# A scan mixer's decay masks from one exponential instead of two, with its vector operands in PSUM

## Chip, cores, metric

One core of a Trainium2 chip runs the whole program. The metric is the device time of one execution in microseconds (us), the median of several runs. Engine names are those of the profile: PE multiplies matrices, PEld loads its weights, DVE is the vector engine, ACT the scalar engine, POOL the GpSimd engine, SP issues DMAs. SBUF is the on-chip memory, PSUM the eight banks of 128 x 512 float32 words that PE writes.

## What is computed

A four-layer trunk over 256 context tokens and 256 latent tokens, model width 1024. Each layer has a mixer and a gated feed-forward block (FFN); mixers are differential attention (layers 0 and 3), windowed attention (layer 1) and a bidirectional state-space scan (layer 2), which the change is about. Cut to that scan, for one direction:

```
xbc = silu(conv5(u @ w_xbc) + bias);  dt = softplus(u @ w_dt + dt_bias)
a_cs = cumsum(dt * A) over each chunk of 128 tokens
chunk_states = einsum(B, exp(a_cs[-1] - a_cs), x * dt)
state = state * exp(a_cs[-1]) + chunk_states
decay_in = exp(where(tril, a_t[..., :, None] - a_t[..., None, :], -inf))
y_diag = einsum(C @ B^T, decay_in, x * dt);  y_off = einsum(C, prev_state, exp(a_cs))
y = (y_forward + flip(y_backward) + x * d_skip) * silu(z)
out = rmsnorm_per_group(y) @ w_out
```

There are 32 heads of width 64 in 4 groups, state width 128, and four chunks (two per stream), forward and backward.

## The kernel before

Every large product is made to float32 accuracy from three matmuls (`lin`, L291 to L293): a weight tile is loaded by SP into `wr`, copied by ACT to `wh` (L264) and its rest is subtracted by POOL into `wl` (L266). A unit of the scan's projection is 24 matmuls of 512 columns into one PSUM bank (tag `mm`).

`ssd_mixer` (L1287) goes over four groups g. In each it makes ten units: two for B and C, four for x (all six go through `conv_silu`, L1076) and four gates z (`gate`, L1310). `conv_silu` copies the bank into the padded tile `xpad` (ACT, L1083), makes the first tap from it (ACT, L1089), adds four taps on DVE (L1097) in an SBUF tile `cw`, and ends with a tanh (ACT, L1100) and a product (DVE, L1102). The steps sizes dt are made once, in `ssd_dt` (L1126), which comes after the latent stream's gates and B, C units; its DVE chain (L1132 to L1146) ends in transposes on PE (L1152).

`ssd_core` (L1181) is called twice per group, for four heads each. It makes x by tokens (`xtok`, L1208); six weighted copies of it (DVE, L1222), from which PE makes the chunk states (L1227, recurrence on DVE, L1232 and L1236); a selector `sel` per direction (DVE, L1213). Then for each of two pairs of heads j, for each head and direction: PE spreads a row of cumulative sums over all partitions (`rb`, L1247), ACT subtracts the token's own sum and clips it by Relu (four instructions, L1256) and takes the exponential (L1259), DVE multiplies by `cd` (L1260), which POOL has made as score x dt (L1250). DVE adds the two directions (L1262), and PE makes the output from it (`yd`, L1266). The states' part is a product and an addition on DVE (L1284, L1285).

The order on each engine is set at build time by a scheduler from the program's order and its own costs, and each engine then runs its list in order. PSUM tags here: `mm` has two banks, to which `ar` is added while no FFN table is in it, and the bank `ad` goes to the tag named by `EXTRA`; `sc` has two, `sm` two. The four tiles `wa` are used by no one in this mixer; the next FFN block's first table rows are loaded into them ahead of it.

Of the kernel before, what the change touches and what calls it, by code (L numbers as in the profile page):

```python
# [180 lines left out]
class Trunk:  # L181
# [4 lines left out]
    DMB = 3  # L186
# [442 lines left out]
    def ffn(self, i, u, streams, pool, gate, after, nxt):  # L629
# [446 lines left out]
    def conv_silu(self, ps, ci, dst, s, pool):  # L1076
# [9 lines left out]
        acc = self.t([P, 2, HALF], "cw", self.CW, pool=pool)[:, :ns]  # L1086
# [5 lines left out]
        if self.ACTTAP:  # L1092
            tm = self.t([P, 2, HALF], "cw", self.CW, pool=pool)[:, :ns]
            nc.scalar.activation(tm, xp[:, s0:s1, 4 : 4 + HALF], AF.Copy, scale=tap(4))
            nc.gpsimd.tensor_tensor(out=acc, in0=acc, in1=tm, op=AL.add)
        for j in range(1, 5 - self.ACTTAP):
# [29 lines left out]
    def ssd_dt(self, ps, pool):  # L1126
# [4 lines left out]
        v, e, q, p = w(), w(), w(), w()  # L1131
# [49 lines left out]
    def ssd_core(self, g, hf, bc, xf, sc, pool):  # L1181
# [33 lines left out]

        prev = [{}, {}]
        for d, order in ((0, (0, 1, 2, 3)), (1, (1, 0, 3, 2))):
            hd = slice(32 * d + h0, 32 * d + h0 + 4)
            st = None
            for n, c in enumerate(order[:3]):  # L1220
                xw = self.t([P, HALF], "v", 4, pool=pool)
                tt(  # L1222
                    out=xw.rearrange("p (h x) -> p h x", h=4), in0=xtok[:, c].rearrange("p (h x) -> p h x", h=4),
                    in1=self.wst[:, c, hd].unsqueeze(2).to_broadcast([P, 4, 64]), op=AL.mult,
                )
# [14 lines left out]
        for j in range(2):  # L1240
            yd = self.psum("sc")
            for hh in (2 * j, 2 * j + 1):
                ms = []
                for d in range(2):
                    hd = 32 * d + h0 + hh
                    rb = self.psum("sc")
                    nc.tensor.matmul(rb, sel[d][:, hh, :], self.rows, start=True, stop=True)  # L1247
                    m = self.t([P, NT], "dm", self.DMB, pool=pool)
                    cd = self.t([P, NT], "cd", self.CDB, pool=pool)
                    getattr(nc, self.ENG_CD).tensor_tensor(  # L1250
                        out=cd.rearrange("p (c l) -> p c l", c=4), in0=cbm[d].rearrange("p (c l) -> p c l", c=4),
# [279 lines left out]
```

## Time and profile before

| what | us |
|---|---|
| median of 3 runs (2724.1 to 2736.1) | 2726.4 |
| the profiled execution: its own time | 2728.9 |
| its span in the profile | 2726.7 |
| PE busy | 2531.5 (93%) |
| DVE busy | 1648.1 (60%) |
| ACT busy | 1234.0 (45%) |
| POOL busy | 1089.7 (40%) |

The mixer of the change lies between about 1360 and 1870 us of the span. The shares above are averages over all layers; for this change the stretches of that mixer are read by themselves. A matmul's duration in the profile includes the time in which the next one already runs, so the pace of PE is read from the starts of successive matmuls.

### The profile page before, as it was taken

How to read it: one execution, taken by the hardware profiler on the slowest of the kernel's cores; microseconds unless marked ns; L12 is line 12 of the kernel's file. 1: busy time of each engine (PE TensorE's matmuls, PEld its weight loads, DVE VectorE, ACT ScalarE, POOL GpSimd, SP SyncE). 2: the span in 40 equal slices, each digit the busy share in tenths (PEclk: the TensorE clock that was granted, in tenths of full speed). 3: DMA queues.
4: the chain of work that ended last, by engine and by line, in shares of the span. 5: the costliest groups of instructions: out<-in, count | busy, mean ns of one | idle time of the engine just before them, and what ended most of it. 6: DMA issues, size and time to landing. Idle time of an engine off the chain costs nothing.

```text
span 2726.7 us, 37430 instructions
## 1 busy us (share of the span) xinstructions
PE 2531.5 (93%) x13570; PEld 2089.7 (77%) x13570; DVE 1648.1 (60%) x3844; ACT 1234.0 (45%) x2514; POOL 1089.7 (40%) x525
## 2 busy tenths in 40 slices
PE   7899999999999999999988888889999998997998
PEld 4777688888776798888876666667988887876997
DVE  3776649931567649921689898866485116667112
ACT  5454553222557653222545565554432225555543
POOL 3322044444321054444243445442544443433784
PEclk9999999999999999999989899999999999999999
DMA  8333437742231147732221111123486323323452
GB/s 319 116 102 122 149 99 260 255 151 93 94 101 47 46 140 263 265 113 94 99 86 39 56 53 60 65 77 108 142 299 239 99 94 104 105 88 130 147 185 78
DMA packets 108040, 353.29 MB, mean 130 GB/s; under 512 B 14032, under 2 KB 24656, under 8 KB 105808
## 3 DMA queue, kind: packets, MB, share of 16 engines
q1 hardware_dynamic: 107280, 349.57, 38.1%
q8 instruction: 107, 1.75, 0.3%
q10 hardware_dynamic: 576, 1.34, 0.1%
q14 instruction: 77, 0.63, 0.1%
HBM read 329.36 MB, written 11.53 MB: 125 GB/s over the span
## 4 chain that ended last, share of the span: by engine, by line
PE 67%; DVE 14%; ACT 5%; issue 3%; DMA 2%; POOL 2%; DVEq 0%; ACTq 0%; SPq 0%; POOLq 0%
PE mm L291 6%; PE mm L292 6%; PE mm L293 6%; PE sc L291 5%; PE sc L293 5%; PE sc L292 5%; PE mm L302 4%; PE mm L303 4%; PE mm L301 4%; DVE dm L1260 2%; DVE cw L1097 2%; PE sc L303 1%; PE sc L301 1%; PE sc L302 1%; POOL wl L266 1%
## 5 line engine op out<-in xcount | busy, mean ns | idle before, releaser
L266 POOL TENSOR_TENSOR wl<-wr,wh 128x1024 fp32r<-128x1024 f32 x356 | 856.1, 2411 | 1354.9 <-ACT wh L264 1216.2
L264 ACT ACTIVATE wh<-wr 128x1024 fp32r<-128x1024 f32 x356 | 377.0, 1061 | 756.8 <-issue 277.1
L291 PE MATMUL mm<-uh,wh 128*128 128x512 f32 (+1 forms) x1136 | 406.5, 358 | 9.0 <-ACT uh L560 8.4
L293 PE MATMUL mm<-uh,wl 128*128 128x512 f32 (+1 forms) x1136 | 406.0, 357 | 0.0
L292 PE MATMUL mm<-ul,wh 128*128 128x512 f32 (+1 forms) x1136 | 405.4, 357 | 0.5 <-DVE sublng L861 0.4
L644 DVE TENSOR_TENSOR sc<-sc,sg 128x512 f32<-128x512 f32 (+1 forms) x100 | 57.5, 575 | 430.0 <-PE sc L293 423.2
L291 PE MATMUL sc<-uh,wh 128*128 128x512 f32 (+1 forms) x800 | 273.0, 341 | 0.7 <-DVE hid L647 0.7
L293 PE MATMUL sc<-uh,wl 128*128 128x512 f32 (+1 forms) x800 | 272.4, 341 | 0.0
L292 PE MATMUL sc<-ul,wh 128*128 128x512 f32 (+1 forms) x800 | 272.4, 340 | 0.0
L291 PEld LDWEIGHTS mm<-uh,wh 128*128 128x128 f32 x1136 | 219.6, 193 | 41.3 <-ACT uh L560 9.0
L292 PEld LDWEIGHTS mm<-ul,wh 128*128 128x128 f32 x1136 | 219.2, 193 | 30.2 <-issue 2.5
L293 PEld LDWEIGHTS mm<-uh,wl 128*128 128x128 f32 x1136 | 219.2, 193 | 27.8 <-issue 1.8
L303 PE MATMUL mm<-wl,hid 128*128 128x512 f32 x444 | 176.1, 397 | 0.0
L301 PE MATMUL mm<-wh,hid 128*128 128x512 f32 x444 | 176.1, 397 | 0.0
L302 PE MATMUL mm<-wh,hid 128*128 128x512 f32 x444 | 175.8, 396 | 0.0
L291 PEld LDWEIGHTS sc<-uh,wh 128*128 128x128 f32 x800 | 152.2, 190 | 17.7 <-DVE hid L647 0.9
L292 PEld LDWEIGHTS sc<-ul,wh 128*128 128x128 f32 x800 | 151.9, 190 | 16.8
L293 PEld LDWEIGHTS sc<-uh,wl 128*128 128x128 f32 x800 | 151.9, 190 | 16.9
L390 DVE SCALAR_TENSOR_TENSOR sq<-wa,sm 128x512 f32<-128x512 f32 x224 | 145.1, 677 | 0.1
L266 POOL TENSOR_TENSOR wl<-wa,wh 128x1024 fp32r<-128x1024 f32 x49 | 117.9, 2406 | 56.4 <-ACT wh L264 56.0
L1250 POOL TENSOR_TENSOR cd<-h,dtt 128x512 f32<-128x512 f32 x64 | 78.6, 1233 | 123.7 <-DVE dm L1260 117.6
L291 PE MATMUL ar<-uh,wh 128*128 128x256 f32 (+1 forms) x352 | 120.6, 343 | 0.0
(415 smaller groups left out, 5735.0 us busy)
## 6 DMA issues: line engine op xcount, KB each, us to landing
wr<-in_fin SPq DMA_DIRECT2D x154, 512.0 KB, 3.5
wa<-in_adat SPq DMA_DIRECT2D x144, 512.0 KB, 4.8
wr<-in_fout SPq DMA_DIRECT2D x77, 512.0 KB, 3.5
wr<-in_ssi SPq DMA_DIRECT2D x40, 512.0 KB, 3.5
wa<-in_adaw SPq DMA_DIRECT2D x36, 512.0 KB, 5.3
wr<-in_daqk SPq DMA_DIRECT2D x24, 512.0 KB, 3.7
wa<-in_fin SPq DMA_DIRECT2D x22, 512.0 KB, 3.5
wr<-in_sso SPq DMA_DIRECT2D x16, 512.0 KB, 3.5
```

Source lines behind the costliest of these rows:

```text
L264: nc.scalar.activation(h, raw, AF.Copy)
L266: eng.tensor_tensor(out=l, in0=raw, in1=f32(h), op=AL.subtract)
L291: mm(out, wh, ah[ka][:, a:b], start=j == 0, stop=False)
L292: mm(out, wh, al[ka][:, a:b], start=False, stop=False)
L293: mm(out, wl, ah[ka][:, a:b], start=False, stop=j == len(todo) - 1)
L301: mm(out, ah[ka][:, tk], wt.h[:, kw, :], start=j == 0, stop=False)
L302: mm(out, al[ka][:, tk], wt.h[:, kw, :], start=False, stop=False)
L303: mm(out, ah[ka][:, tk], wt.l[:, kw, :], start=False, stop=j == len(todo) - 1)
L390: nc.vector.scalar_tensor_tensor(out=self.t([P, D], "sq", 2)[:, :512], in0=w[:, x, :], scalar=1.0, in1=self.arows[r, x], op0=AL.mult, op1= ...
L644: nc.vector.tensor_tensor(out=pu[:, :w], in0=pu[:, :w], in1=sg[:, :w], op=AL.mult)
L1097: nc.vector.scalar_tensor_tensor(out=acc, in0=xp[:, s0:s1, j : j + HALF], scalar=tap(j), in1=acc, op0=AL.mult, op1=AL.add)
L1250: getattr(nc, self.ENG_CD).tensor_tensor(out=cd.rearrange("p (c l) -> p c l", c=4), in0=cbm[d].rearrange("p (c l) -> p c l", c=4), in1=sel ...
```

## The change

Four things are done together. (1) In `conv_silu` and `gate` the accumulator and the gate's value stay in the PSUM bank of the projection; the gate's factor 0.5 moves into the product `gated`. (2) `ssd_dt` keeps one temporary in PSUM, also makes `nacs`, the negated sums, and is called right after the latent stream's dt projection, ahead of its gates. (3) In `ssd_core` the weighted copies of x are made straight from the transposes' PSUM bank, 128 to 384 columns at a time, into two `wa` tiles; the selector of a head is one column of `pick`, repeated by the access pattern, and for a pair of heads a small tile made by ACT. (4) Per head, not per head and direction: ACT subtracts for both directions (one into SBUF, one in place in PSUM), DVE takes the minimum of the two, ACT one exponential, DVE one product with `cd`, for which POOL now makes both directions' products and adds them. The two heads' `yd` matmuls come after both. The bank `ad` goes from `mm` to `sc`.

```diff
-    DMB = 3
+    DMB = 4
-    EXTRA = ('sm', 'sc', 'mm')
+    EXTRA = ('sm', 'sc', 'sc')
...
-        acc = self.t([P, 2, HALF], "cw", self.CW, pool=pool)[:, :ns]
+        acc = ps[:, : ns * HALF].rearrange("p (s t) -> p s t", s=ns)
...
+        self.pick = self.t([P, 64], "pick", 1, F32R, pool=pool)
+        nc.vector.tensor_copy(self.pick, self.cst["ident2"])
...
-        v, e, q, p = w(), w(), w(), w()
+        v, e, p = w(), w(), w()
+        q = ps[:64]
...
+        nc.scalar.activation(self.nacs, acv, AF.Copy, scale=-1.0)
...
+        xw = [self.t([P, 2, 512], "wa", self.ADA_T).rearrange("p a (b x) -> p (a b) x", b=2) for _ in range(2)]
         for j in range(2):
             tp = self.psum("sm")
...
+            tv = tp.rearrange("p (c h x) -> p c h x", c=4, h=2)
             nc.scalar.activation(xtok[:, :, j * P : (j + 1) * P], tp.rearrange("p (c x) -> p c x", c=4), AF.Copy)
-        sel = []
-        for d in range(2):
-            t = self.t([P, 4, P], "sel", 2, F32R, pool=pool)
-            hd = 32 * d + h0
-            nc.vector.tensor_copy(t, self.cst["ident2"][:, hd : hd + 4].unsqueeze(2).to_broadcast([P, 4, P]))
-            sel.append(t)
+            for d in range(2):
+                hd = 32 * d + h0 + 2 * j
+                for cs in ((slice(0, 3),) if d == 0 else (slice(0, 2), slice(3, 4))):
+                    n = cs.stop - cs.start
+                    tt(
+                        out=xw[d][:, cs, j * P : (j + 1) * P].rearrange("p c (h x) -> p c h x", h=2), in0=tv[:, cs],
+                        in1=self.wst[:, cs, hd : hd + 2].unsqueeze(3).to_broadcast([P, n, 2, 64]), op=AL.mult,
+                    )
...
-            yd = self.psum("sc")
+            ms = {}
             for hh in (2 * j, 2 * j + 1):
...
+                for d, o in enumerate((cd, m)):
+                    eng.tensor_tensor(
+                        out=o.rearrange("p (c l) -> p c l", c=4), in0=cbm[d].rearrange("p (c l) -> p c l", c=4),
+                        in1=self.dtt[:, :, hd[d] : hd[d] + 1].to_broadcast([P, 4, P]), op=AL.mult,
+                    )
+                eng.tensor_tensor(out=cd, in0=cd, in1=m, op=AL.add)
+
+                rb = [self.psum("sc") for _ in range(2)]
                 for d in range(2):
+                    nc.tensor.matmul(
+                        rb[d], self.pick[:, hd[d] : hd[d] + 1].to_broadcast([P, P]), self.rows, start=True, stop=True
                     )
-                    for c in range(4):
-                        t = slice(c * P, (c + 1) * P)
-                        nc.scalar.activation(
-                            m[:, t], rb[:, t], AF.Relu, scale=-1.0, bias=self.acs[:, c, hd : hd + 1]
-                        )
-                    nc.scalar.activation(m, m, AF.Exp, scale=-1.0)
-                    tt(out=m, in0=m, in1=cd, op=AL.mult)
-                    ms.append(m)
-                getattr(nc, self.ENG_MADD).tensor_tensor(out=ms[0], in0=ms[0], in1=ms[1], op=AL.add)
+                f = self.t([P, NT], "tf", 2, pool=pool)
                 for c in range(4):
                     t = slice(c * P, (c + 1) * P)
+                    nc.scalar.activation(f[:, t], rb[0][:, t], AF.Identity, bias=self.nacs[:, c, hd[0] : hd[0] + 1])
+                    nc.scalar.activation(
+                        rb[1][:, t], rb[1][:, t], AF.Identity, bias=self.nacs[:, c, hd[1] : hd[1] + 1]
+                    )
+                tt(out=rb[1], in0=rb[1], in1=f, op=AL.min)
+                nc.scalar.activation(rb[1], rb[1], AF.Exp)
+                tt(out=m, in0=rb[1], in1=cd, op=AL.mult)
+            yd = self.psum("sc")
...
+                two = self.t([P, 2, 64], "sel", 2, F32R, pool=pool)
+                nc.scalar.activation(two, self.cst["ident2"][:, hd : hd + 2].unsqueeze(2).to_broadcast([P, 2, 64]), AF.Copy)
...
-                    tt(out=er[:, t], in0=yo[:, t], in1=er[:, t], op=AL.mult)
-                    getattr(nc, self.ENG_YO).tensor_tensor(out=x[:, t], in0=x[:, t], in1=er[:, t], op=AL.add)
+                    tt(out=yo[:, t], in0=yo[:, t], in1=er[:, t], op=AL.mult)
+                    tt(out=x[:, t], in0=yo[:, t], in1=x[:, t], op=AL.add)
...
-            nc.scalar.activation(z[:, a:b], ps[:, :w], AF.Copy, scale=0.5)
             nc.scalar.activation(th[:, :w], ps[:, :w], AF.Tanh, scale=0.5)
             nc.vector.scalar_tensor_tensor(
-                out=z[:, a:b], in0=th[:, :w], scalar=1.0, in1=z[:, a:b], op0=AL.add, op1=AL.mult
+                out=z[:, a:b], in0=th[:, :w], scalar=1.0, in1=ps[:, :w], op0=AL.add, op1=AL.mult
             )
...
                     project_dt(wd, s)
+                    if s == "l":
+                        self.ssd_dt(pdt, pool)
...
-                self.ssd_dt(pdt, pool)
```

The scheduler's lists move at three places that matter below. The first is DVE's list where the step sizes dt are made (`cw` are temporaries, `sc` or `ad` the bank of the projection, `bc` the tile of C). Before, and then with the change:

```order
L1097 SCALAR_TENSOR_TENSOR cw_13112<-xpad_2553_12687,cwt_12672,cw_13112 128x256 x4
L1102 SCALAR_TENSOR_TENSOR bc_12691<-cw_13113,cw_13112 128x256
L1097 SCALAR_TENSOR_TENSOR cw_13147<-xpad_2552_12684,cwt_12672,cw_13147 128x256 x4
L1132 TENSOR_SCALAR cw_13156<-sc_12690,dtp_12674 64x512
L1102 SCALAR_TENSOR_TENSOR bc_12692<-cw_13148,cw_13147 128x256
L1133 SCALAR_TENSOR_TENSOR cw_13157<-cw_13156 64x512
```

```order
L1327 SCALAR_TENSOR_TENSOR o_86<-cw_12870,mm_12845 128x256
L1091 SCALAR_TENSOR_TENSOR mm_12873<-xpad_2553_12688,cwt_12671,mm_12873 128x256 x4
L1096 SCALAR_TENSOR_TENSOR bc_12692<-cw_12899,mm_12873 128x256
L1091 SCALAR_TENSOR_TENSOR ar_12907<-xpad_2552_12685,cwt_12671,ar_12907 128x256 x4
L1130 TENSOR_SCALAR cw_12965<-ad_12691,dtp_12673 64x512
L1096 SCALAR_TENSOR_TENSOR bc_12693<-cw_12933,ar_12907 128x256
L1131 SCALAR_TENSOR_TENSOR cw_12966<-cw_12965 64x512
```

The dt chain (L1132, now L1130) stood behind the latent stream's B and C units (`bc`, second time round); now it stands behind the context stream's, and the latent stream's four gates and two units come after its start.

The second is DVE's list while a unit of x is convolved and a call of `ssd_core` runs (`cw` or `mm` the convolution's accumulator, `dm`, `cd`, `sm`, `sc` the core's tiles, `o` the output). Before, and with the change:

```order
L1097 SCALAR_TENSOR_TENSOR cw_13608<-xpad_2552_12684,cwt_12672,cw_13608 128x512
L1285 TENSOR_TENSOR o_86<-o_86,dm_13449 128x256
L1260 TENSOR_TENSOR dm_13459<-dm_13459,cd_13460 128x512
L1097 SCALAR_TENSOR_TENSOR cw_13608<-xpad_2552_12684,cwt_12672,cw_13608 128x512
L1336 TENSOR_TENSOR o_86<-o_86 128x512
L1260 TENSOR_TENSOR dm_13470<-dm_13470,cd_13471 128x512
L1097 SCALAR_TENSOR_TENSOR cw_13608<-xpad_2552_12684,cwt_12672,cw_13608 128x512
L1262 TENSOR_TENSOR dm_13459<-dm_13459,dm_13470 128x512
L1102 SCALAR_TENSOR_TENSOR o_86<-cw_13609,cw_13608 128x512
```

```order
L1091 SCALAR_TENSOR_TENSOR mm_13561<-xpad_2552_12685,cwt_12671,mm_13561 128x512
L1294 TENSOR_TENSOR o_86<-sm_13425,o_86 128x256
L1268 TENSOR_TENSOR dm_13436<-ad_13442,cd_13437 128x512
L1091 SCALAR_TENSOR_TENSOR mm_13561<-xpad_2552_12685,cwt_12671,mm_13561 128x512
L1266 TENSOR_TENSOR sc_13463<-sc_13463,tf_13466 128x512
L1293 TENSOR_TENSOR sm_13492<-sm_13492,tf_13496 128x384
L1091 SCALAR_TENSOR_TENSOR mm_13561<-xpad_2552_12685,cwt_12671,mm_13561 128x512
L1268 TENSOR_TENSOR dm_13457<-sc_13463,cd_13458 128x512
L1293 TENSOR_TENSOR sm_13504<-sm_13504,tf_13508 128x128
L1091 SCALAR_TENSOR_TENSOR mm_13561<-xpad_2552_12685,cwt_12671,mm_13561 128x512
L1341 SCALAR_TENSOR_TENSOR o_86<-o_86 128x512
L1279 SCALAR_TENSOR_TENSOR o_86<-o_86,sng_12674,ad_13478 128x512
```

In both lists the core's instructions stand between the taps of one unit; with the change the bank `mm` of the unit is in use until the row behind the last one shown, its final product L1096.

The third is SP's list of DMAs at the end of the mixer, with the change (`yspill` holds the finished groups, `hspill` the residual, `in_sso` the output weights, `in_adat` the next FFN block's table):

```order
L260 DMA wr_16710<-in_sso 128x1024
L373 DMA wa_17741<-in_adat 128x1024
L373 DMA wa_17743<-in_adat 128x1024
L373 DMA wa_17745<-in_adat 128x1024
L1400 DMA cw_16378<-yspill 128x512
L373 DMA wa_17747<-in_adat 128x1024
L1400 DMA cw_16382<-yspill 128x512
```

Before, these four loads of `in_adat` stood in the FFN block of layer 1, ahead of this mixer; now `wa` is taken by the weighted copies until the mixer's last states are made.

## Rows read from the trace of the kernel before

**Rows 1.** Windows of the mixer: busy us and instructions per engine, PE clock, DMA.
```profile
1360.00:1428.00 68.00, 61.22 (x389) 54.24 (x388) 52.28 (x56) 28.49 (x53) 28.46 (x12) 0.90 0.25 79
1428.00:1812.00 384.00, 318.14 (x1466) 242.38 (x1465) 337.59 (x504) 212.98 (x495) 162.57 (x100) 0.93 0.18 58
1812.00:1870.00 58.00, 51.57 (x248) 40.69 (x249) 32.04 (x55) 29.63 (x65) 22.66 (x14) 0.97 0.38 130
```

**Rows 2.** Waits of PE, 1428 to 1812: total us, times, longest.
```profile
PE sc L1266 <- DVE dm L1262: 32.1, 22, 6.9
```

**Rows 3.** Groups of DVE's instructions, 1428 to 1812: busy us, mean ns, idle before.
```profile
L1097 DVE SCALAR_TENSOR_TENSOR cw<-xpad,cwt,cw 128x512 f32<-128x512 f32 x81 | 78.8, 973 | 1.5 <-ACT cw L1089 0.6
L1260 DVE TENSOR_TENSOR dm<-dm,cd 128x512 f32<-128x512 f32 x58 | 62.2, 1076 | 21.7 <-ACT dm L1259 18.9 <-POOL cd L1250 2.7
L1262 DVE TENSOR_TENSOR dm<-dm,dm 128x512 f32<-128x512 f32 x29 | 37.2, 1283 | 0.1
L1222 DVE TENSOR_TENSOR v<-h,wst 128x256 f32<-128x256 f32 x48 | 28.3, 620 | 0.8 <-PE sm L1227 0.4 <-ACT h L1208 0.3
...
L1102 DVE SCALAR_TENSOR_TENSOR o<-cw,cw 128x512 f32<-128x512 f32 x15 | 13.1, 872 | 2.1 <-ACT cw L1100 2.1
...
L1285 DVE TENSOR_TENSOR o<-o,dm 128x384 f32<-128x384 f32 x14 | 12.0, 854 | 0.0
...
L1213 DVE CAST sel<-cst_ssd 128x512 fp32r<-128x512 f32 x14 | 10.3, 736 | 2.8 <-PE sc L1274 2.7
```

**Rows 4.** Lines L1284, L1285, 1340 to 1900: ns min/median/max, first and last start.
```profile
L1284 DVE TENSOR_TENSOR dm<-sm,dm x48: 275/414/553, 1446.0 to 1845.1; 128x384 f32<-128x384 f32 x16, 128x128 f32<-128x128 f32 x16, 128x256 f32<-128x256 f32 x16
L1285 DVE TENSOR_TENSOR o<-o,dm x48: 276/415/2612, 1449.8 to 1845.6; 128x384 f32<-128x384 f32 x16, 128x128 f32<-128x128 f32 x16, 128x256 f32<-128x256 f32 x16
```

**Rows 5.** Timeline near 1611: start us, us, engine, line.
```profile
1611.34 2.83 POOL L266 TENSOR_TENSOR wl<-wr,wh 128x1024 fp32r<-128x1024 f32 x1
...
1611.85 2.87 DVE L1260 TENSOR_TENSOR dm<-dm,cd 128x512 f32<-128x512 f32 x1
```

**Rows 6.** Prices elsewhere: three lines' minimum/median/maximum ns, two groups' busy us, mean ns.
```profile
L1271 DVE SCALAR_TENSOR_TENSOR o<-o,sng,sc x16: 734/746/748, 1449.0 to 1843.6; 128x512 f32<-128x512 f32 x16
...
L594 DVE TENSOR_TENSOR mm<-mm,o x11: 684/689/700, 695.7 to 2700.4; 128x512 f32<-128x512 f32 x11
...
L1340 POOL TENSOR_TENSOR sq<-sq x12: 1267/1292/3026, 1479.6 to 1847.5; 128x512 f32<-128x512 f32 x12
...
L1259 ACT ACTIVATE dm<-dm 128x512 f32<-128x512 f32 x57 | 36.5, 640 | 0.7
...
L1256 ACT ACTIVATE dm<-sc,acs 128x128 f32<-128x128 f32 x226 | 65.3, 372 | 46.5 <-PE sc L1247 44.1 <-DVE o L1285 2.4
```

**Rows 7.** PE's timeline: wide matmuls in an FFN block, two left out; eight narrow ones.
```profile
2099.53 0.39 PE L293 MATMUL mm<-uh,wl 128*128 128x512 f32 x1
...
2100.21 0.39 PE L293 MATMUL mm<-uh,wl 128*128 128x512 f32 x1
...
1605.19 1.09 PE L1266 MATMUL sc<-dm,h 128*64 128x128 f32 x8 [0.27 <-DVE dm L1262]
```

**Rows 8.** Groups of PE's wide matmuls, 1428 to 1812, one of three lines each.
```profile
L293 PE MATMUL mm<-uh,wl 128*128 128x512 f32 x120 | 51.3, 427 | 0.0
...
L293 PE MATMUL ad<-uh,wl 128*128 128x512 f32 x60 | 25.2, 419 | 0.0
...
L293 PE MATMUL ar<-uh,wl 128*128 128x512 f32 x56 | 23.5, 420 | 0.0
```

**Rows 9.** PE's timeline where the step sizes are made.
```profile
1410.00 0.69 PE L1152 MATMUL sm<-cst_base,cw 64*128 64x64 f32 x4 [6.78 <-DVE cw L1145]
```

**Rows 10.** Convolution's tanh and copies on ACT, 1428 to 1812.
```profile
L1089 ACT ACTIVATE cw<-xpad,cbt,cwt 128x512 f32<-128x512 f32 x20 | 16.3, 816 | 0.0
...
L1100 ACT ACTIVATE cw<-cw 128x512 f32<-128x512 f32 x21 | 13.4, 638 | 30.2 <-DVE cw L1097 30.2
...
L1083 ACT ACTIVATE xpad<-mm 128x512 f32<-128x512 f32 x9 | 5.3, 589 | 0.1
```

More of the change, by code (lines that the diff above doesn't have):

```diff
@@ L1091, in conv_silu @@
         )
[L1092 to L1096, printed above, removed]
+        for j in range(1, 5):
             nc.vector.scalar_tensor_tensor(
@@ L1147, in ssd_dt @@
         one = lambda n: self.t([P, 4, 64], n, pool=pool)
-        self.dtt, at, self.acs, self.wst, self.dec = one("dtt"), one("at"), one("acs"), one("wst"), one("dec")
+        self.dtt, self.acs, self.nacs, self.wst, self.dec = (one(n) for n in ("dtt", "acs", "nacs", "wst", "dec"))
+        at = one("at")
         for src, dst in ((v, self.dtt), (e, at)):
@@ L1220, in ssd_core @@
             for n, c in enumerate(order[:3]):
[L1221 to L1224, printed above, removed]
-                )
                 ps = self.psum("sm")
-                nc.tensor.matmul(ps[:, :HALF], sc["btok"][:, c * P : (c + 1) * P], xw, start=True, stop=True)
+                nc.tensor.matmul(ps[:, :HALF], sc["btok"][:, c * P : (c + 1) * P], xw[d][:, c], start=True, stop=True)
                 new = sc["st"][:, (3 * d + n) * HALF : (3 * d + n + 1) * HALF]
@@ L1240, in ssd_core @@
         for j in range(2):
-            yd = self.psum("sc")
+            ms = {}
             for hh in (2 * j, 2 * j + 1):
-                ms = []
-                for d in range(2):
[L1245 to L1251, printed above, removed]
-                        in1=self.dtt[:, :, hd : hd + 1].to_broadcast([P, 4, P]), op=AL.mult,
-                    )
-                    for c in range(4):
-                        t = slice(c * P, (c + 1) * P)
-                        nc.scalar.activation(
-                            m[:, t], rb[:, t], AF.Relu, scale=-1.0, bias=self.acs[:, c, hd : hd + 1]
-                        )
-                    nc.scalar.activation(m, m, AF.Exp, scale=-1.0)
-                    tt(out=m, in0=m, in1=cd, op=AL.mult)
-                    ms.append(m)
-                getattr(nc, self.ENG_MADD).tensor_tensor(out=ms[0], in0=ms[0], in1=ms[1], op=AL.add)
-                r = 64 * (hh % 2)
@@ new lines, in ssd_core @@
+                hd = [32 * d + h0 + hh for d in range(2)]
+                m = ms[hh] = self.t([P, NT], "dm", self.DMB, pool=pool)
+                cd = self.t([P, NT], "cd", self.CDB, pool=pool)
+                eng = getattr(nc, self.ENG_CD)
+                for d, o in enumerate((cd, m)):
[3 more added lines that the diff above has]
+                    )
@@ L1266, in ssd_core @@
+                tt(out=rb[1], in0=rb[1], in1=f, op=AL.min)
+                nc.scalar.activation(rb[1], rb[1], AF.Exp)
+                tt(out=m, in0=rb[1], in1=cd, op=AL.mult)
+            yd = self.psum("sc")
+            for c in range(4):
+                t = slice(c * P, (c + 1) * P)
+                for hh in (2 * j, 2 * j + 1):
+                    r = 64 * (hh % 2)
                     nc.tensor.matmul(
-                        yd[r : r + 64, t], xtok[:, c, 64 * hh : 64 * hh + 64], ms[0][:, t], start=True, stop=True,
+                        yd[r : r + 64, t], xtok[:, c, 64 * hh : 64 * hh + 64], ms[hh][:, t], start=True, stop=True,
@@ L1273, in ssd_core @@
                 rb = self.psum("sc")
-                nc.tensor.matmul(
-                    rb, sel[d].rearrange("p h x -> p (h x)")[:, 256 * j + 64 : 256 * j + 192], self.rows, start=True, stop=True
-                )
+                two = self.t([P, 2, 64], "sel", 2, F32R, pool=pool)
+                hd = 32 * d + h0 + 2 * j
+                nc.scalar.activation(two, self.cst["ident2"][:, hd : hd + 2].unsqueeze(2).to_broadcast([P, 2, 64]), AF.Copy)
+                nc.tensor.matmul(rb, two.rearrange("p h x -> p (h x)"), self.rows, start=True, stop=True)
                 yo = self.psum("sm")
@@ L1331, in ssd_mixer @@
             zs = self.o[4 * ((g + 1) % 2) : 4 * ((g + 1) % 2) + 4]
-            for n in range(self.ZB):
-                zs[n] = self.t([P, NT], "zs", self.ZB, pool=pool)
             def gated(n):
-                getattr(nc, self.ENG_GATE).tensor_tensor(out=xg[n], in0=xg[n], in1=zs[n], op=AL.mult)
+                nc.vector.scalar_tensor_tensor(
+                    out=xg[n], in0=xg[n], scalar=0.5, in1=zs[n], op0=AL.mult, op1=AL.mult
+                )
                 d = 2 * (n > 0)
```

12 lines of the change are left out of this document (4 added, 8 removed).

## Prediction

> **What bounds the kernel now.** PE is busy in almost every slice of the program, but the change touches one mixer, so I read that stretch by itself, by windows [rows 1]. It falls into a start (1360 to 1428), where the step sizes dt are made, a middle (1428 to 1812), where the scan's calls run beside the projection, and an end (1812 to 1870). In the middle the busiest engine is DVE: 337.6 of 384 us, 88%. [...] The waits of PE come next: half of its idle time, 32.1 us, ends with the sum of the two directions' masks on DVE [rows 2].
>
> How much of PE's 384 us is work? In an FFN block, where PE is held up by nothing, three wide matmuls start within 0.68 us, one per 0.227, though each is shown as 0.39 long [rows 7]. The middle has three lines of 120, 60 and 56 wide matmuls [rows 8], 708 in all, so 161 us. The other 758 of its 1466 instructions [rows 1] are mostly narrow; eight took 1.09 us [rows 7], so I estimate 758 x 0.136 = 103. PE's floor is about 264 us, 69% of the middle. PE could be much faster there, if DVE let it.
>
> Then the groups of DVE [rows 3]. Something is odd in them: a product of 512 columns takes 1.08 or 1.28 us on average, where another 512-column operation takes 0.69 [rows 6]. A pair of lines shows why [rows 4]: L1284 and L1285 have the same widths and the same minimum (0.275 and 0.276), but the one with an input in PSUM never exceeds 0.553, while the one with both inputs in SBUF goes to 2.612. The timeline shows such a case: a DVE product of 2.87 us beside a POOL subtraction of 2.83, both ending at about 1614 [rows 5]. So DVE's operations on two SBUF inputs wait for POOL here, those with one in PSUM don't.
>
> **The change, part by part, in the middle.** All prices for PSUM operands are taken from [rows 4, 6].
> - Taps: 81 x (0.973 - 0.746, the price of L1271, which also has a column as scalar) = 18.4 us less on DVE.
> - Final products of the convolution: 15 x (0.872 - 0.69) = 2.7 less. Gates gain a little too; I leave it out.
> - Masks: 58 products and 29 sums cost 62.2 + 37.2 = 99.4; now 29 minima and 29 products, each with one PSUM input, 58 x 0.69 = 40.0. 59.4 less.
> - Weighted copies: still 48, with widths 128, 256 and 384, so the median of L1284, 0.414: 28.3 - 19.9 = 8.4 less.
> - Selectors: 10.3 go from DVE. ACT gets two small copies per pair of heads, at 0.372 or so, 28 x 0.372 = 10 more.
> - Additions of the states' part, of 384 columns: 14 x (0.854 - 0.553) = 4.2 less.
>
> Sum on DVE: 103.4, from 337.6 to about 234.
>
> [...]
>
> ACT: one exponential less per head, 29 x 0.640 = 18.6 less, a copy less per gate, the selectors more; the 128-column subtractions are as many as before, half of them now in place in PSUM, which no row of this mixer shows; between the price of L1256 (0.372) and half as much again it is 0 to 21 us. ACT stays near 210 of 384: cover, not bound. POOL gets 29 sums at 1.29 [rows 6], 37 us, and stands at 200 instead of 163, with less to wait for from DVE. PE has the same matmuls; a repeated column instead of a written selector changes what is loaded, not how much, and I cost it at nothing, since weight loads lie beside the matmuls (PEld is busy for 242 of 384).
>
> So after the change PE is the busiest with 264. It won't reach 100%: lists are fixed, and each engine waits in order. Before, the bounding engine ran at 88% of the middle and PE's floor was 69% of it. I take 81%, nearer the upper of these two, because no other engine stands above three quarters then: 264 / 0.81 = 326, **58 us less**. The ends: 88% gives 300 (84 less), 73% gives 362 (22 less).
>
> **The start.** The dt chain on DVE stood behind all of the stretch's work, and PE waited 6.8 us for it [rows 9]; the clock of 0.90 in these 68 us is another 6.8. The change starts the chain earlier, with four gates and two units of PE's work behind it, 144 matmuls of 256 columns, about 16 us at half the wide price. In the order shown DVE's gates are put between its steps, so it ends later by these. I take half of the 13.6: **7 us less**, range 0 to 13.6.
>
> **The end.** Four table loads of 512 KB now stand on SP ahead of the spilled groups, behind the last weighted copies' readers. The DMA share there is 0.38, so two thirds of the engines' time is free, and the residual's reload behind them waits for the core's last matmuls anyway. If they go through late, the output projection is late by their transfer. PE can gain at most its 6.4 idle us here. I put 0, between -6 and +5.
>
> Sum: 2728.9 (the profiled execution) - 58 - 7 = 2664. That execution is 2.5 above the median, so **2661**.
>
> **Rivals.**
> 1. *PE hardly waits* (chance 0.17). All bounds at their good end: 84 + 13.6 + 6.4, or 2728.9 - 104 - 2.5 = 2622. For it: DVE, ACT and POOL all have slack. Against: PE reached such a share nowhere in this mixer.
> 2. *The longer chain takes over* (0.18). One head now needs eight subtractions, minimum, exponential and product in a row, before PE may make `yd`. Before it was four subtractions, exponential, product and sum: roughly 4 x 0.28 us more and as many hand-overs. If the 32.1 us of waits for the mask stay, and only the rest goes, the gain is half of the 65: 2728.9 - 33 - 2.5 = 2693. For it: that wait is PE's largest. Against: DVE's part in it ends sooner, and ACT has three banks of `sc` instead of two to work ahead in.
> 3. *POOL is late with weights* (0.07), no change: POOL's list has 37 us more ahead of the subtractions that make `wl`. If each of some 30 weights came 2.2 us late, 65 us are gone, and it stays at 2726. Against: 163 of 384 is a light load.
> 4. *Slower* (0.08): a bank of `mm` is no longer free after one copy, but after copy, first tap (0.59 + 0.82), four taps, tanh (0.64) and product [rows 10]: 1.41 + 4 x 0.746 + 0.64 + 0.69 = 5.7 us, and there are three banks, not four. Two units on the other banks cover 2 x 24 x 0.227 = 10.9. In the order shown eight core operations stand between taps and product, some 4.7 us, so 10.4 of 10.9 are used up, and the core's own matmuls give only some more cover. If DVE falls behind, PE waits at each of the 20 units. From 65 / 20 = 3.3 us per unit the gain is lost; at 5 us the time is 2728.9 - 65 + 100 - 2.5 = 2761.
>
> That the change doesn't do what it says (PSUM operands wait for POOL too) would need other maxima than those shown [rows 4].
>
> **How the numbers follow.** The forecast's own range, 2640 to 2685, has 0.50; with rivals 1 to 4 that makes 1. About 0.5% (13.6 us) is what a measurement of this kernel tells from no change. Faster by more: 0.50 + 0.17 + 0.18 = 0.85; within it: 0.07; slower: 0.08. The range leaves out rivals 3 and 4: from 2620, just below rival 1, to 2705, just above the middle at 73% with nothing from the start (2728.9 - 22 - 2.5 = 2704).
>
> **What would show it.** Right: the mixer's middle shrinks from 384 to about 326 us; DVE busy there near 234, its taps at 0.75 and minima and products at 0.69 with maxima below 0.8; PE's wait for the mask below 15 us, clock above 0.95; the 6.8 us before L1152's successor down to a few. Wrong: taps above 0.9, PE waiting for `mm` banks (rival 4), for `wl` (3), or as long as before for the product that `yd` needs (2); or a change of time outside of the mixer.

## The result, and the profile after

The changed kernel takes 2653.1 us (median of 4 runs, 2648.2 to 2657.1) beside 2725.2 before: ratio 0.9726, 95% interval 0.9696 to 0.9757. Measured once more later, beside other kernels, it gave 0.9726 again, interval 0.9707 to 0.9745 (2650.0 beside 2728.0). So it is 72 to 78 us faster; 2661 was forecast. The profiled execution took 2648.2, its span 2646.2: 80.5 us less than the span before, some 7 of which lie in the choice of the two executions (one 2.5 above its median, the other 5 below).

Windows of the mixer after the change, with the columns of [rows 1]. They are cut near the places in PE's instructions at which the windows of before were cut (the middle holds 31 instructions more than the window of before):

```profile
1360.00:1424.00 64.00, 56.57 (x367) 49.99 (x366) 45.45 (x68) 31.52 (x67) 31.25 (x18) 0.89 0.23 75
1424.00:1735.00 311.00, 290.04 (x1497) 224.49 (x1497) 244.88 (x464) 198.74 (x499) 190.34 (x131) 0.99 0.24 79
1735.00:1790.00 55.00, 52.14 (x247) 41.60 (x247) 22.80 (x39) 21.34 (x34) 21.08 (x9) 1.00 0.47 158
```

The gain is where it was expected: the middle went from 384 to 311 us, DVE there from 337.6 to 244.9, the clock from 0.93 to 0.99. Measured between equal numbers of PE's instructions (13570 in both programs; cut behind 6855, 7242, 8707 and 8955 of them, where the windows of before begin and end), the start went from 68.0 to 67.7 us (7 us less forecast), the middle from 385.0 to 304.2 (58 less forecast) and the end from 57.1 to 53.7 (0 forecast). The expectations below still count with 73 us for the middle, the difference of the two windows.

That is 84.5 us in this mixer, 4 more than the whole program gained. Some 5 us went the other way outside of it: PE's instructions 10950 to 11450, from the end of the following FFN block into the mixer of layer 3, take 95.9 us instead of 91.2 (96.4 in the second run of the changed kernel). The prediction names a change of time outside of the mixer as a sign of being wrong, and it had not foreseen this one; the run with the eighth bank below shows what it goes with.

DVE's groups in the middle:

```profile
L1091 DVE SCALAR_TENSOR_TENSOR mm<-xpad,cwt,mm 128x512 f32<-128x512 f32 x52 | 38.6, 750 | 2.8 <-ACT mm L1087 2.5
L1232 DVE TENSOR_TENSOR h<-h,dec 128x256 f32<-128x256 f32 x32 | 25.0, 780 | 2.2 <-ACT h L1230 1.9
...
L1216 DVE TENSOR_TENSOR wa<-sm,wst 128x384 f32<-128x384 f32 (+2 forms) x42 | 15.1, 416 | 0.9 <-ACT h L1211 0.9
L1266 DVE TENSOR_TENSOR sc<-sc,tf 128x512 f32<-128x512 f32 x20 | 13.9, 695 | 4.0 <-ACT sc L1263 2.5 <-ACT tf L1262 1.2
...
L1341 DVE SCALAR_TENSOR_TENSOR o<-o 128x512 f32<-128x512 f32 x15 | 13.3, 894 | 0.1
L1268 DVE TENSOR_TENSOR dm<-sc,cd 128x512 f32<-128x512 f32 x19 | 13.1, 689 | 10.6 <-POOL cd L1252 8.4 <-ACT sc L1267 2.0
```

Set beside [rows 3]: taps 0.973 to 0.750, mask products 1.076 to 0.689, sums of 1.283 replaced by minima of 0.695, weighted copies 0.620 to 0.416. Two lines with two SBUF inputs, L1232 (the product of a state with its decay) and L1341 (the gated product), are not among what I priced. L1232 became slower; this was its row before, 1428 to 1812:

```profile
L1232 DVE TENSOR_TENSOR h<-h,dec 128x256 f32<-128x256 f32 x32 | 18.0, 562 | 2.5 <-ACT h L1230 2.5
```

What is left of PE's waits, in the mixer, largest first (total us, times, longest):

```profile
PE sc L1274 <- DVE dm L1268: 6.0, 4, 2.1
PE ad L1274 <- DVE dm L1268: 4.5, 2, 2.3
PE mm L288 <- DVE o L1327: 4.2, 1, 4.2
...
PE sm L1151 <- DVE cw L1143: 3.2, 1, 3.2
```

The wait for the mask, 32.1 us in [rows 2], is 10.5. The third and fourth rows stand in the start.

### The profile page after: what moved, and what is told of

Same layout as the page of the kernel before. It is cut to its first block, busy times and chain, and to the rows that moved or that the text cites. A ratio compares the mean times of both kernels' runs of the same rounds, so it can differ in the third digit from the quotient of the medians.

```text
span 2646.2 us, 37378 instructions
## 1 busy us (share of the span) xinstructions
PE 2495.8 (94%) x13570; PEld 2065.5 (78%) x13570; DVE 1538.5 (58%) x3797; ACT 1212.5 (46%) x2495; POOL 1113.6 (42%) x557
## 5 line engine op out<-in xcount | busy, mean ns | idle before, releaser
L263 POOL TENSOR_TENSOR wl<-wr,wh 128x1024 fp32r<-128x1024 f32 x356 | 852.5, 2401 | 1339.2 <-ACT wh L261 1224.8
L288 PE MATMUL mm<-uh,wh 128*128 128x512 f32 (+1 forms) x1184 | 423.7, 358 | 11.7 <-ACT uh L557 6.9
L289 PE MATMUL mm<-ul,wh 128*128 128x512 f32 (+1 forms) x1184 | 423.0, 357 | 0.6 <-DVE sublng L858 0.6
L290 PE MATMUL mm<-uh,wl 128*128 128x512 f32 (+1 forms) x1184 | 421.7, 356 | 0.0
L288 PEld LDWEIGHTS mm<-uh,wh 128*128 128x128 f32 x1184 | 228.2, 193 | 45.0 <-ACT uh L557 7.1
L289 PEld LDWEIGHTS mm<-ul,wh 128*128 128x128 f32 x1184 | 227.6, 192 | 30.4 <-issue 1.8
L290 PEld LDWEIGHTS mm<-uh,wl 128*128 128x128 f32 x1184 | 227.7, 192 | 29.9 <-issue 2.3
L298 PE MATMUL mm<-wh,hid 128*128 128x512 f32 x454 | 180.1, 397 | 0.9 <-DVE o L675 0.9
L299 PE MATMUL mm<-wh,hid 128*128 128x512 f32 x454 | 179.7, 396 | 0.0
L263 POOL TENSOR_TENSOR wl<-wa,wh 128x1024 fp32r<-128x1024 f32 x49 | 117.7, 2403 | 59.7 <-ACT wh L261 57.0
L288 PE MATMUL ar<-uh,wh 128*128 128x256 f32 (+1 forms) x400 | 134.8, 337 | 1.9 <-ACT uh L557 1.9
L289 PE MATMUL ar<-ul,wh 128*128 128x256 f32 (+1 forms) x400 | 135.6, 339 | 0.0
```

Of the source, the lines that this page charges most:

```text
L263: eng.tensor_tensor(out=l, in0=raw, in1=f32(h), op=AL.subtract)
L288: mm(out, wh, ah[ka][:, a:b], start=j == 0, stop=False)
L289: mm(out, wh, al[ka][:, a:b], start=False, stop=False)
L290: mm(out, wl, ah[ka][:, a:b], start=False, stop=j == len(todo) - 1)
L298: mm(out, ah[ka][:, tk], wt.h[:, kw, :], start=j == 0, stop=False)
L299: mm(out, al[ka][:, tk], wt.h[:, kw, :], start=False, stop=False)
```

## The experiments

Time differences below are differences of ratios to the kernel before (each with runs of that kernel on its own chip), times 2728 us, against the changed kernel's 0.9726.

**One exponential or two.** The masks of before in the changed kernel, and so without the sum of the two products on POOL; all else stays.

```diff
-                rb = [self.psum("sc") for _ in range(2)]
...
-                tt(out=rb[1], in0=rb[1], in1=f, op=AL.min)
-                nc.scalar.activation(rb[1], rb[1], AF.Exp)
-                tt(out=m, in0=rb[1], in1=cd, op=AL.mult)
...
+                            m[:, t], rb[:, t], AF.Relu, scale=-1.0, bias=self.acs[:, c, hd : hd + 1]
...
+                    nc.scalar.activation(m, m, AF.Exp, scale=-1.0)
+                    tt(out=m, in0=m, in1=cd, op=AL.mult)
+                    ms.append(m)
+                nc.vector.tensor_tensor(out=ms[0], in0=ms[0], in1=ms[1], op=AL.add)
```

> The changed kernel with the masks of before: per head two Relus by four pieces, two exponentials, two products and one sum in SBUF. In the trace of the change DVE's time in the middle fell by 92.7 us (337.6 to 244.9) and the middle became 73 us shorter, 0.79 us for each us of DVE. Theory T (the middle follows DVE's load, wherever it lies): 58 products at 1.08 and 29 sums at 1.28 come back for 29 minima at 0.69 and 29 products at 0.69: 62.6 + 37.1 - 40 = 60 us more on DVE, 47 of the time: about 2700, with a wait of PE for the mask of over 20 us. Rival M (only the shorter chain of the mask counts, the other parts nothing): nearly all of the gain is gone, 2715 to 2725. Rival C (the gain is that of the convolution's operands and the earlier dt): under 20 us more, below 2673.

Measured: 2698.1, ratio 0.9893 (0.9876 to 0.9909): 46 us of the gain gone, where T said 47. M's 2715 lies outside, C's 2673 too. Two groups of DVE in this kernel, 1424 to 1740, products and sums:

```profile
L1262 DVE TENSOR_TENSOR dm<-dm,cd 128x512 f32<-128x512 f32 x55 | 54.3, 989 | 2.4 <-POOL cd L1252 1.3 <-ACT dm L1261 1.0
...
L1264 DVE TENSOR_TENSOR dm<-dm,dm 128x512 f32<-128x512 f32 x28 | 38.1, 1360 | 0.0
```

PE's wait for the mask is back at 22.8 us (16.3 and 6.5, by two banks). The run doesn't separate what fewer operations and what their place give; the one with the mask's product in SBUF, below, gives a part of the second.

**The convolution's accumulator back in SBUF.**

```diff
-        acc = ps[:, : ns * HALF].rearrange("p (s t) -> p s t", s=ns)
+        acc = self.t([P, 2, HALF], "cw", self.CW, pool=pool)[:, :ns]
```

> The changed kernel with the convolution's accumulator in SBUF as before (the gates' stays in PSUM). T: 81 taps at 0.97 instead of 0.75 and 15 finals at 0.87 instead of 0.68, 21 us more on DVE, by 0.79 some 16 us: about 2669. Rival M: the taps' operands don't matter, 2648 to 2658. Rival B (the mm banks held through five operations cost time, as in my rival 4): the banks are free after one copy again, so it becomes faster, 2640 to 2648.

Measured: 2690.1, ratio 0.9861 (0.9843 to 0.9878): 37 us slower, more than twice T's 16; M and B fall. First the taps of this kernel, then those of the changed kernel: ns as minimum/median/maximum, in all of the program.

```profile
L1091 DVE SCALAR_TENSOR_TENSOR cw<-xpad,cwt,cw x104: 472/752/2865, 1363.7 to 1740.2; 128x512 f32<-128x512 f32 x88, 128x256 f32<-128x256 f32 x16
```

```profile
L1091 DVE SCALAR_TENSOR_TENSOR mm<-xpad,cwt,mm x68: 472/749/757, 1360.7 to 1689.4; 128x512 f32<-128x512 f32 x60, 128x256 f32<-128x256 f32 x8
```

Medians alike, maxima 2.865 and 0.757. Groups of DVE in this kernel, 1424 to 1740:

```profile
L1091 DVE SCALAR_TENSOR_TENSOR cw<-xpad,cwt,cw 128x512 f32<-128x512 f32 x80 | 107.0, 1337 | 0.9 <-ACT cw L1087 0.2
...
L1341 DVE SCALAR_TENSOR_TENSOR o<-o 128x512 f32<-128x512 f32 x12 | 14.6, 1218 | 0.1
```

T priced a tap at its mean of before, 0.973. It is 1.337 here. POOL is now busy for 61% of the middle (191 of the 311 us from 1424 to 1735); before it was 163 of 384 (42%) [rows 1]. So a tap meets POOL more often: of the 88 taps of 512 columns, 59 ran beside a POOL instruction here, 31 of them beside a subtraction of `wl` (now L263); before it was 20 and 12. The timeline shows one such meeting (start, us, engine, line):

```profile
1626.58 2.56 POOL L263 TENSOR_TENSOR wl<-wr,wh 128x1024 fp32r<-128x1024 f32 x1
1626.82 2.87 DVE L1091 SCALAR_TENSOR_TENSOR cw<-xpad,cwt,cw 128x512 f32<-128x512 f32 x1
```

And the same meeting in the changed kernel, where the accumulator lies in PSUM:

```profile
1599.47 2.40 POOL L263 TENSOR_TENSOR wl<-wr,wh 128x1024 fp32r<-128x1024 f32 x1
1599.73 0.75 DVE L1091 SCALAR_TENSOR_TENSOR mm<-xpad,cwt,mm 128x512 f32<-128x512 f32 x1
```

All of them together, by the start and end of each instruction in the traces of both kernels: the 31 taps beside L263 took 2.04 us on average with the accumulator in SBUF, 25 such taps 0.75 with it in PSUM; with POOL idle it is 0.75 in both. Of the 31, POOL had started first in 20; these took 2.51 on average, each 0.20 us less than what was left of POOL's instruction plus 0.75. In the rows above 2.32 of POOL's 2.56 us were left, and the tap took 2.87, 0.20 less than 2.32 + 0.75. So these 20 took as long as if each had waited until 0.20 us before the end of POOL's instruction, and then worked its 0.75.

**The convolution alone.** The kernel before, with only the accumulators of convolution and gates in PSUM.

```diff
-        acc = self.t([P, 2, HALF], "cw", self.CW, pool=pool)[:, :ns]
+        acc = ps[:, : ns * HALF].rearrange("p (s t) -> p s t", s=ns)
...
-            nc.scalar.activation(z[:, a:b], ps[:, :w], AF.Copy, scale=0.5)
...
-                out=z[:, a:b], in0=th[:, :w], scalar=1.0, in1=z[:, a:b], op0=AL.add, op1=AL.mult
+                out=z[:, a:b], in0=th[:, :w], scalar=1.0, in1=ps[:, :w], op0=AL.add, op1=AL.mult
...
```

> The kernel before, with only the accumulators of the convolution and of the gates in PSUM (no ACT copy of the gate, the 0.5 moved to the gated product). T: 81 taps at 0.75 instead of 0.97, finals at 0.68 instead of 0.87: 21 us less on DVE, by 0.79 some 17 of time, ratio about 0.994 to the kernel before. Rival D (what one edit saves is partly lost again, since the two-SBUF operations that stay wait for POOL all the same and POOL's share rises): under 10 us, ratio over 0.996. Rival S (as the run that took this edit back cost 37 us): 37 us, ratio 0.986. My rival 4 (banks of mm held): slower, over 1.

Measured: 2707.9, ratio 0.9921 (0.9909 to 0.9934): 22 us faster; D, S and rival 4 lie outside, and T's 0.994 just misses the interval. So the convolution's accumulator in PSUM is worth 22 us alone (with the gates) and 37 beside the other parts. Between equal numbers of PE's instructions the middle is 28 us shorter than before (385.0 to 356.8), but the start is 3 longer and the end 5. Its taps, 1424 to 1735, those with the tag `mm`:

```profile
L1097 DVE SCALAR_TENSOR_TENSOR mm<-xpad,cwt,mm 128x512 f32<-128x512 f32 x36 | 26.9, 748 | 1.0 <-ACT mm L1089 0.6
```

But once PE waits 9.7 us for a bank that only the final product of a convolution frees (longest wait, in the start):

```profile
PE ad L291 <- DVE o L1102: 9.7, 1, 9.7
```

That is the mechanism of the prediction's rival 4, in one place; it may be part of why the edit gives less alone.

**Where an operand lies, instructions equal.** In one kernel only the mask's product reads SBUF, in another only the weighted copies.

```diff
-                tt(out=rb[1], in0=rb[1], in1=f, op=AL.min)
-                nc.scalar.activation(rb[1], rb[1], AF.Exp)
-                tt(out=m, in0=rb[1], in1=cd, op=AL.mult)
+                tt(out=f, in0=rb[1], in1=f, op=AL.min)
+                nc.scalar.activation(f, f, AF.Exp)
+                tt(out=m, in0=f, in1=cd, op=AL.mult)
```

> The changed kernel with as many instructions, but the minimum written to SBUF, the exponential in place there, and so the mask's product on two SBUF operands; the bank is free one step earlier. T: the 29 products go from 0.69 to about 1.08, 11 us more on DVE, some 9 us of time: about 2662; maxima of the product above 2 us. Rival M (fewer operations is what counts, not where they lie): within 3 us of 2653, with the product still near 0.69.

```diff
-                        out=xw[d][:, cs, j * P : (j + 1) * P].rearrange("p c (h x) -> p c h x", h=2), in0=tv[:, cs],
+                        out=xw[d][:, cs, j * P : (j + 1) * P].rearrange("p c (h x) -> p c h x", h=2), in0=xtok[:, cs, j * P : (j + 1) * P].rearrange("p c (h x) -> p c h x", h=2),
```

> The changed kernel with the weighted copies read from the SBUF copy of the transposed inputs, not from the bank. T: 48 copies from 0.416 to about 0.62, up to 10 us more on DVE, some 7 of time: about 2660. Rival M: within 3 us of 2653. Against T speaks that these copies may lie where POOL does nothing; then their mean stays below 0.5 and the time too.

Measured: 2666.5, ratio 0.9772 (0.9755 to 0.9788), 13 us slower (T: 9); and 2665.2, ratio 0.9767 (0.9752 to 0.9781), 11 slower (T: 7). M falls twice. The product (1424 to 1740), then the copies (1424 to 1735), in their kernels:

```profile
L1268 DVE TENSOR_TENSOR dm<-tf,cd 128x512 f32<-128x512 f32 x28 | 26.8, 956 | 14.7 <-POOL cd L1252 11.8 <-ACT tf L1267 2.1 <-POOL sq L1347 0.3
```

```profile
L1216 DVE TENSOR_TENSOR wa<-h,wst 128x384 f32<-128x384 f32 (+2 forms) x45 | 35.3, 841 | 1.5 <-ACT h L1211 1.4
```

0.689 became 0.956, and 0.416 became 0.841, without an instruction more. Both kernels free a bank earlier than the changed kernel does, which by itself would speak for faster, not slower.

**Less work on POOL.** One of the two products per head, and the sum, go from POOL's list, so that kernel leaves out the backward direction's weights:

```diff
-                for d, o in enumerate((cd, m)):
+                for d, o in ((0, cd),):
...
-                eng.tensor_tensor(out=cd, in0=cd, in1=m, op=AL.add)
```

> The changed kernel with less work on POOL: the second direction's product of the score matrix with dt and the sum of the two are left out (so the backward direction's weights are missing from the masks), some 70 us of POOL's 190 in the middle; DVE has the same instructions. If DVE's two-SBUF operations wait for POOL: the state product falls from 0.78 to below 0.6, the gated product from 0.89 to below 0.8, at unchanged means of the operations with a PSUM operand (0.75, 0.69); time 5 to 15 us less. If they are slow for another reason (DMA, ACT), their means stay.

Measured: 2640.1, ratio 0.9681 (0.9664 to 0.9699), 12 us faster, POOL 121 us in the middle instead of 190. The gated product came out as expected, 0.89 to 0.77, at 0.748 for the taps and 0.685 to 0.688 for the mask's product. My number for the state product was missed: its mean only fell from 0.78 to 0.75. Its median fell from 0.657 to 0.425:

```profile
L1232 DVE TENSOR_TENSOR h<-h,dec x32: 407/425/2193, 1425.7 to 1712.1; 128x256 f32<-128x256 f32 x32
```

By the start and end of each instruction, 16 of 32 now run with POOL idle (7 of 32 in the changed kernel, 23 before), and in all three kernels such a one takes 0.41 to 0.43 us, never more. Of the other 16, four meet L263 (1.80 each; four in the changed kernel too, 1.66) and 12 the product that I left in (0.83). These make the mean. So it is POOL's work beside them that makes these operations slow; POOL's share of the time alone doesn't give the price, as it is 39% here, less than the 42% of before, when the mean was 0.562. DVE is at 1534.5 us in the whole program, 2 less than in the second run of the changed kernel, so the 12 us are not DVE's time: more likely the wait for `cd`, which went with the sum: DVE's idle time before the mask's product is 4.5 us here, 4.2 of them for ACT, beside 16.2 in the changed kernel, 11.8 of them for `cd` (8.4 in the row above, 3.4 in that of the other bank). That was not tried apart.

**The start.** The dt chain at its place of before:

```diff
-                    if s == "l":
-                        self.ssd_dt(pdt, pool)
...
+                self.ssd_dt(pdt, pool)
```

> The changed kernel with the dt chain at its place of before, behind all gates. T: the wait for the chain goes back from 3.2 to about 6.8 us and the wait of the projection for the gate's bank (4.2 us) goes, so the time is within 4 us of the changed kernel's. Rival E (the early dt is worth the 7 us predicted): 5 to 10 us slower, ratio to the kernel before 0.9745 to 0.9765.

Measured: 2645.4, ratio 0.9696 (0.9682 to 0.9709), 8 us *faster* than the changed kernel; both expectations missed. First the changed kernel's window of 1380 to 1400, then this one's:

```profile
1380.00:1400.00 20.00, 16.80 (x118) 15.46 (x118) 11.06 (x15) 5.95 (x13) 4.97 (x2) 0.69 0.23 76
```

```profile
1380.00:1400.00 20.00, 19.54 (x99) 16.36 (x97) 16.17 (x23) 9.52 (x16) 10.84 (x5) 1.00 0.43 141
```

With the chain late, PE waits 0.2 us for it, not 3.2, and its granted clock in these 20 us is 1.00; with the chain early it is 0.69: read by the microsecond it is 0.50 to 0.52 from 1379 to 1382 and from 1389 to 1399, about where the two waits of 4.2 and 3.2 us end (1378.0 and 1389.8). The wait for the gate's bank is gone too. One of 3.0 us for a bank that a convolution's final product frees has come instead, later in the start:

```profile
PE mm L288 <- DVE o L1096: 3.0, 1, 3.0
```

The whole start takes 61.6 us instead of 67.7.

The changed kernel's DVE timeline shows what stands ahead of the gate:

```profile
1374.74 1.48 DVE L1138 TENSOR_TENSOR ad<-cw 64x512 f32<-64x512 f32 x1
...
1377.58 0.40 DVE L1327 SCALAR_TENSOR_TENSOR o<-cw,mm 128x256 f32<-128x256 f32 x1
...
1387.07 2.71 DVE L1143 SCALAR_TENSOR_TENSOR cw<-cw,cw 64x512 f32<-64x512 f32 x1
```

A gate's product, which now frees its `mm` bank, stands behind steps of the chain (the wait of 4.2), and some of the chain's own steps have two SBUF inputs (2.71 us for one; the same step takes 0.68 with the chain late).

**A copy to free the gates' banks.**

```diff
+            src = ps[:, :w]
+            if s == "l":
+                src = z[:, a:b]
+                nc.scalar.activation(src, ps[:, :w], AF.Copy)
...
-                out=z[:, a:b], in0=th[:, :w], scalar=1.0, in1=ps[:, :w], op0=AL.add, op1=AL.mult
+                out=z[:, a:b], in0=th[:, :w], scalar=1.0, in1=src, op0=AL.add, op1=AL.mult
```

> The changed kernel, with the first stream's gates copied out of their bank by ACT (8 copies more, 4 of them in the start), so that the projection need not wait until DVE has made the gate. T: the 4.2 us wait at the start goes and the time falls by about 4, ratio to the kernel before 0.971. Rival: the wait moves to the dt chain or to the next list entry, within 2 us of the changed kernel.

Measured: 2656.9, ratio 0.9728 (0.9714 to 0.9742), no change. The edit copies the latent stream's gates, four in all and all in the start, not the first stream's eight as I wrote. The wait of 4.2 is gone, but PE waits 2.6 us for ACT's tanh (L1330), which is now the bank's last reader, and still 3.5 for the chain: the rival.

**The eighth bank.**

```diff
-    EXTRA = ('sm', 'sc', 'sc')
+    EXTRA = ('sm', 'sc', 'mm')
```

> The changed kernel with the eighth bank given to the projection, as before, not to the masks. If the third bank for the masks is what lets ACT work ahead: 8 to 20 us slower, with waits of PE or ACT for sc. If the projection's banks, held through the convolution, are what costs (my rival 4): up to 10 us faster. Between: within 3 us.

Measured: 2641.8, ratio 0.9680 (0.9667 to 0.9693), 12 us faster, a little more than "up to 10" that rival 4's cause was given. The wait for a gate's bank is 1.4 us instead of 4.2, and that for the mask 1.3 instead of 10.5, although the masks have a bank fewer; the second I had not expected and can't explain:

```profile
PE mm L288 <- DVE o L1327: 1.4, 1, 1.4
PE sc L1274 <- DVE dm L1268: 1.3, 4, 0.6
```

Between equal numbers of PE's instructions, the start is 3.6 us shorter than in the changed kernel, the middle 2.5, and the stretch into layer 3's mixer (above) 3.5. That stretch takes 90.6 to 92.6 us in all five kernels with the bank at `mm` (the one before among them), and 95.0 to 96.7 in all nine with it at `sc`. So some 3.5 us of the gain lie where the argument of rival 4 doesn't reach; how the choice of the bank in this mixer comes to matter in the next one is open.

**Together.** The changed kernel as it is, with late dt and the bank, and with the first state read from PSUM besides:

```diff
+                src = ps[:, :HALF]
...
-                        out=new.rearrange("p (h x) -> p h x", h=4), in0=st.rearrange("p (h x) -> p h x", h=4),
+                        out=new.rearrange("p (h x) -> p h x", h=4), in0=last.rearrange("p (h x) -> p h x", h=4),
...
+                last = src if n == 0 else new
```

> The changed kernel itself once more, beside the others of this call. Ratio to the kernel before 0.9726 as measured, within 0.970 to 0.976.

> The changed kernel with both edits that made it faster: dt chain late, eighth bank with the projection. If they act at different places (the start; the bank waits of the whole middle): 8 + 12 us, ratio 0.965. If both only clear the start (the bank alone took a wait of 4.2 us for the gate away there, the late dt too): as the better of the two, 0.968 to 0.970.

> As late_mm, and the first of the two state products in a row reads the state from its PSUM bank, so 16 of 32 products with two SBUF operands (0.78 us on average, minimum 0.41) have one in PSUM. T: 16 x (0.78 - 0.42) = 6 us less on DVE, by 0.79 some 4 of time. Rival: the wait for POOL moves to the other products and the sm bank is held longer, within 2 us of late_mm or slower.

Measured: 2650.0, ratio 0.9726 (0.9707 to 0.9745); 2639.5, ratio 0.9680 (0.9663 to 0.9697); 2635.9, ratio 0.9665 (0.9650 to 0.9680). The two edits don't add up: together they give what the bank gives alone. The start is then free of idle time,

```profile
1360.00:1424.00 64.00, 64.00 (x430) 56.85 (x429) 43.03 (x71) 32.77 (x59) 30.64 (x14) 1.00 0.29 99
```

but the middle takes 306.8 us instead of the 301.7 with the bank alone, and PE waits 8.8 us for the mask in it instead of 1.3; why, stays open. The last kernel's state products:

```profile
L1233 DVE TENSOR_TENSOR h<-h,dec 128x256 f32<-128x256 f32 x16 | 17.8, 1113 | 0.0
...
L1233 DVE TENSOR_TENSOR h<-sm,dec 128x256 f32<-128x256 f32 x16 | 6.6, 415 | 1.9 <-ACT h L1231 1.9
```

The 16 that read PSUM take 0.415. The 4 us against late_mm agree with T, but the intervals overlap. Against the changed kernel this version is 14 (by medians) to 17 us (by ratios) faster, with intervals apart. It has the lowest median of all, though it isn't told apart from the other two with the bank.

## Why the prediction was right, and where its sizes were off

**The bound and the mechanism.** DVE bounded the middle, by operations that were slow beside POOL (in the kernel before, 12 taps of 512 columns beside the subtraction of `wl` took 2.05 us on average, the 68 with POOL idle 0.74), and PE went faster when they were gone (its clock 0.99 instead of 0.93). The changes of DVE's busy time in the whole program (one profiled execution each) and of the time go together wherever operands or operations of DVE are changed:

| kernel, against | DVE us | time us |
|---|---|---|
| changed (second run), against before | -112 | -75 |
| two exponentials, against changed | +59 | +46 |
| convolution in SBUF, against changed | +58 | +37 |
| weighted copies in SBUF, against changed | +27 | +11 |
| product in SBUF, against changed | +18 | +13 |
| convolution alone, against before | -55 | -22 |

0.4 to 0.8 us of time for each us of DVE. It is no law: with less work on POOL the time fell by 12 us at 2 us less of DVE, with the eighth bank by 12 at 8 more of DVE. The three edits taken back one by one (46 + 37 + 11 = 94) cost more than all of them gave (75). A reason that the traces show is that what is left in SBUF meets POOL more often in the shorter middle (taps at 1.337 instead of 0.973); whether it is all of it was not tried.

**DVE's terms**, in all of the mixer (1340 to 1900):

| term | forecast for the middle | measured |
|---|---|---|
| taps | -18.4 | 96.9 to 73.4 |
| final products | -2.7 | 24.2 to 16.7 |
| gates | left out | 21.6 to 11.5 |
| masks | -59.4 | 110.3 to 44.2 |
| weighted copies | -8.4 | 28.3 to 17.4 |
| selectors | -10.3 | 12.6 to 0 |
| additions of the states' part | -4.2 | 24.8 to 19.3 |
| state product, gated product | not seen | 29.8 to 38.9 |

The prices were right (taps 0.75, minima and products 0.69, maxima of the minima 0.700), and the taps' medians are 749 ns from PSUM beside 752 from SBUF. In the middle DVE came to 245, not 234: the two lines not seen have two SBUF inputs and cost 10 us more there (28.4 to 38.3), as more of them meet POOL (25 of the 32 state products, 9 before), whose share the change raises from 42% to 61%.

**The middle's size**, -81 for -58: the term that was mis-sized is "I take 81%". PE's floor of 264 us in the measured 304.2 is 87%, near the good end of 88% that the prediction gives. The floor itself was a rough one: of the "other 758" instructions 133 have 512 columns too (L1247 56, L1274 28, L301 to L303 49), which at 0.227 each are 12 us more than at 0.136; with them it is 277 and the share 91%. The wait for the mask fell to 10.5 (below the 15 given) and the clock rose to 0.99. The total is off by only 8 us where the middle alone is off by 23: the start's 7 us failed, some 5 us were lost on the way into layer 3's mixer, and the profiled execution lies 5 below its kernel's median. That is luck.

**The start**, -0.3 for -7: "The change starts the chain earlier, [...] I take half of the 13.6" had the wrong sign. In the run with the late chain the wait of 6.8 us is 0.2 without an earlier start, by the rest of the change, and the start is 6.4 us shorter than before; starting early costs some 8 us.

**ACT** stayed cover, as estimated: subtractions in place in PSUM took 0.358, just below the lower bound given, those into SBUF 0.387, and ACT is at 199 us in 311. **The end**: -3.4 for 0, within its bounds.

**The rivals.** 1: PE is still idle for 21 of 311 us in the middle, half of it for the mask. 2: the mask's wait didn't stay. 3: no wait for `wl` among PE's largest. 4 was not the outcome, but its cause is real: the convolution alone shows a wait of 9.7 us of its kind, and another bank for the projection gives 12 us, of which some 6 lie in this mixer's start and middle.

## What to carry to other kernels

Before counting DVE's operations, look at the maxima of those with two SBUF inputs beside a busy POOL: leaving one operand in PSUM, where the matmul put it, took a quarter to a half off the mean of each group tried here (taps 1.337 to 0.750 us, weighted copies 0.841 to 0.416, the mask's product 0.956 to 0.689), without changing their number. The price of those that stayed rose when the rest became faster (0.562 to 0.780 for the state product), so price them by how many of them will run beside POOL's work after the change and beside which of it (in the changed kernel a state product took 1.66 beside the subtraction of `wl`, 0.42 with POOL idle), not by their mean before. And keeping an accumulator in its bank lengthens the bank's life (with the convolution alone PE waited 9.7 us for one bank): try the spare bank at the producer, and look at what else stands ahead of the releasing operation on its engine.

## What was not expected of the hardware

- In the changed kernel a DVE operation of 0.41 us (L1232) took up to 2.26 us, five times its own time, beside a POOL subtraction of 2.4 us; taps with one input in PSUM never took more than 0.757.
- ACT's 512-column exponential in place in PSUM took 0.599 us (L1267), in SBUF 0.640 [rows 6].
- The gain of one edit depended on the others: 22 us alone, 37 beside them.
